# A fused decoder layer in float32: laying out the staging tiles of the up and the down projection, and ending the sums of the down weights earlier

## The chip, the cores and the metric

The kernel runs on one core of a Trainium2 chip. The metric is the device time of one execution of the whole layer in microseconds (us), lower being better. Six actors matter below: TensorE (PE, the matrix products), VectorE (DVE), ScalarE (ACT), GpSimd (POOL), SyncE (SP, which here only issues transfers), and the 16 DMA engines that carry the transfers. Each engine works through its own list of instructions in order and stands at the first one whose condition isn't met.

## The reference

One layer of a decoder for 2048 tokens of width 1024, all in float32. What the change touches is the gated MLP in the middle of it; the lines ahead of it write the `h` that it reads.

```python
h = h + jnp.concatenate([att, pool], axis=-1) @ w_out[i]      # output projection
hn = _rmsnorm(h, ln_ffn[i])
up = _causal_dwconv(hn @ w_up[i], conv_w[i], conv_b[i])       # up stage, 1024 -> 2 x 2816
gate, val = jnp.split(up, 2, axis=-1)
h = h + (jax.nn.silu(gate) * val) @ w_down[i]                 # down stage, 2816 -> 1024
g = jax.nn.sigmoid(_rmsnorm(h, ln_ple[i]) @ w_ple_gate[i])    # gate stage
h = h + g * (p[i] @ w_ple[i])
```

## The kernel before

**Products.** Every float32 operand is split into a high part (a cast on ACT, L84) and a low part (a subtraction on DVE, L85), and a product is three passes of PE: high by high, high by low, low by high (L89 to L91). Both projections of the MLP further save an eighth of the products by a scheme of seven products of half size in place of eight; its operands are sums and differences of quarters of the matrices, named `a11`, `a12`, `a22`, `s1` to `s4` on the side of the activations and `b11`, `b21`, `b22`, `t1` to `t4` on the side of the weights.

**Output projection.** It runs ahead of the up stage. Its mix tiles (`mh`, `ml`) are the moving operand of the products `o` (L89 to L91); the last group walks eight steps `k`, twelve products to a step. Its staging tiles `xc` (tag `xh1`) take the new `h` and are written out to memory.

**Up stage.** It has 44 turns of about 19 us: 2 halves of the tokens times 22 column blocks `f`. A turn makes seven products of twelve matmuls each (L1395), into the PSUM banks `ua`, `ub` and `uc`; the last of a turn is `s4`, and the product `a22` of a turn is made at the head of the next, ahead of that turn's `s2`. The program is written turn by turn, and within the `with tc.manual_schedule` block all engines execute in the order of the text. What stands in it besides the products:

- `raw_load` (L1061, L1065) fetches the weights of a turn as two raw tiles on SP's queue; the second of them lies in the tile `raw2`.
- `Refill.fetch` (L1435) loads operands that an earlier stage left in memory, into `nt` and `ninv` tiles, also on SP's queue; `Refill.take` (L1451, L1452) splits them on ACT and DVE. At the head of the stage six such loads, for `a12` and `s3`, stand right behind the raw weights of turn 1.
- Conv, Silu and the multiplication with the other half (`yv`, `uv`, `ug`, `yg`, L1661 for the multiplication) run one turn behind the products. `results` writes the quarter sums out; `x` and `x2` are its temporaries in tag `dg`. `keep` (L1478) puts most of these writes on SP, the last turn's on GpSimd.
- `down_sums` (L1518) makes, for each of 11 `q`, four sums of the down weights on GpSimd, an operation and a write each (L1530, L1531); the down stage reads them from memory. They are spread over the later turns, by slots, of which a turn has seven.
- `first_units` (L1462, L1465) prepares the first five units of the down stage inside the last turns, from tiles of the up stage's own pools.

**Down stage.** 154 units: 2 halves times 7 products times 11 `q`. A unit needs one weight tile `rw` (L1710) and one activation tile `ra` (L1712), 256 KB each, loaded on SP's queue, and the splits of both (`w` tiles, `ah`, `al`; L84, L85); then PE makes 12 products `dn`. `ahead` loads and splits up to four units beyond the present one, with four buffers of `rw` and of `ra` and seven of `ah` and `al`. The old `h` tiles are loaded by GpSimd (L1756) and the finished sums added to them on DVE (L1764). Only PE's order is that of the text here; the loop is the scheduler's otherwise.

**Where tiles lie.** A tile pool hands out memory by tags: all tiles of a tag share a fixed number of rotating buffers, and the tags of a pool lie one behind the other in the order in which they are first asked for. A pool that opens where an earlier one closed takes over its bytes, and with `reuse_waits="tile"` each new tile then waits for the last users of the very bytes that it lies on, not for the whole old pool. So the place of a tag decides what its first tiles wait for. A tile named `first`, asked for and not used, fixes the place of its tag. Three pools follow each other on the same bytes: the one of the output projection, `fb` of the up stage (with `opb`, the split operands `s3`, `a22` and `a12`, behind it from the other side) and `fd` of the down stage. In KB from their common start:

| pool | tags in order, with the first KB of each |
|---|---|
| output projection | `xh1` 0, mix tiles 20, output weights (`xw`) 52, `sq` 76, `dg` 78, end 82 |
| `fb` | `halo` 0, `yv` 0.75, `uv` 4.75, `dg` 8.75, `t4` 12.75, `raw2` 14.75, `nt` 22.75, `inv` 30.75, `t13` 34.75, `ug` 38.75, `yg` 46.75, end 54.75 |
| `opb` | `s3` 55.25, `a22` 71.25, `a12` 87.25, end 103.25 |
| `fd` | `dacc` 0, `rw` 4, `ra` 12, `ah` 20, `al` 34, `h` 48, `sq` 84, `dg` 86, `inv` 90, `nt` 92, end 96 |

Of the kernel before, what the change touches and what calls it, by code (L numbers as in the profile page):

```python
# [10 lines left out]
F32 = mybir.dt.float32  # L11
F32R = mybir.dt.float32r
# [5 lines left out]
P = 128  # L18
# [7 lines left out]
NF = FF // P  # L26
CH = 512
# [939 lines left out]
def phase_rest(tc, g, mxs, mx, last_pair, xT, pT, w_out, w_up, w_down, w_gate, w_ple, outT):  # L967
# [3 lines left out]
    with ExitStack() as ctx:  # L971
# [72 lines left out]
        NP = NF // 2  # L1044
        turns = [(half, f) for half in range(2) for q in range(NP) for f in (q, q + NP)]
        fb = None
# [323 lines left out]
        fb = fctx.enter_context(tc.tile_pool(name="c_f", bufs=1, reuse_waits="tile"))  # L1370
# [3 lines left out]
        for pool, tag, n, bufs in (  # L1374
            (fb, "yv", 1024, 1),
            (fb, "uv", 1024, 1),
            (fb, "dg", CH, 2),
            (fb, "t4", CH, 1),
            (fb, "raw2", 1024, 2),
            (fb, "nt", CH, 4),  # L1380
            (fb, "inv", CH, 2),
            (fb, "t13", 1024, 1),
            (opb, "s3", CH, 8),
            (opb, "a22", CH, 8),
            (opb, "a12", CH, 8),
        ):
            pool.tile([P, n], F32R if tag == "dg" or pool is opb else F32, tag=tag, bufs=bufs, name="first")
# [123 lines left out]
        def due_sums():  # L1511
            for e in sums[:]:
                e[0] -= 1
                if e[0] < 0:
                    sums.remove(e)
                    e[1]()

        def down_sums(q):  # L1518

            b = []  # L1520
            for r in (w_down[q * P : (q + 1) * P, :], w_down[(q + NP) * P : (q + NP + 1) * P, :]):
                for x in range(2):
                    t = fb.tile([P, CH], F32, tag="nt", bufs=4, name="nt")
                    nc.gpsimd.dma_start(t, r[:, x * CH : (x + 1) * CH])
                    b.append(t)

            def one(n):
                b11, b12, b21, b22 = b
                o, x, y = ((b11, b12, b11), (b12, b22, b12), (b22, b22, b11), (b21, b21, b22))[n]
                nc.gpsimd.tensor_tensor(o, x, y, op=ALU.subtract)  # L1530
                nc.gpsimd.dma_start(g.dd[q][("t1", "t3", "t2", "t4")[n]], o)  # L1531

            return one

        with tc.manual_schedule(engines=set(EN.values())):
# [8 lines left out]
            unit = {}  # L1544
            for i in range(len(turns) + 1):
                over = i == len(turns)
# [10 lines left out]
                def after(slot):  # L1557

                    if i == 0 and 0 < slot or i == NF - 1 and slot > 0 or i in (NF, NF + 1):
                        refill.take(2 + (i == 0 and slot == 1))  # L1560
                    if i == 3 and slot == 4:
                        prep.extend(prepare(1, fb, prep, 4))
                    if prep and (i == 3 or (i, slot) == (4, 0) or (7 * i + slot) % 3 == 0):
                        prep.pop(0)()
                    m = 7 * (i - NF - 2) + slot
                    if m >= 0 and not over:
                        q, at = divmod(m, 14) if m < 14 * (NP - 2) else (i - 2 * NF + NP, slot)
                        wide = m < 14 * (NP - 2)
                        if at == 0:
                            unit["sum"] = down_sums(q)  # L1570
                        for x in range(4):
                            if at == ((2, 5, 8, 11) if wide else (2, 3, 4, 5))[x]:
                                unit["sum"](x)
                    due_sums()

                def splits(slot):
# [12 lines left out]
                if prev:  # L1589
                    nc.scalar.copy(prev.uv[:, lo_], prev.a)  # L1590
                    prev.yv = fb.tile([P, 1024], F32, tag="yv", name="yv")
                    conv_a(prev.yv, prev.uv, NF + prev.f)
                after(0)
                keep_t(i + 1)

# [9 lines left out]
                if over:  # L1605
                    unit[3]()
                after(1)
                if last:
                    for n in range(2):
# [5 lines left out]
                if prev and not over:  # L1615
                    add(prev.ug[:, hi_], prev.c)
                splits(2)
                after(2)
                if last:
                    unit[0]()  # L1620
# [61 lines left out]
        psd = dctx.enter_context(tc.tile_pool(name="c_psd", bufs=1, space=PSUM, reuse_waits="tile"))  # L1682
        fd = dctx.enter_context(tc.tile_pool(name="c_fd", bufs=1, reuse_waits="tile"))
        aux[0] = fd

        SEQ = (
            ("a11", "b11", True, True, (0, 0)),
# [237 lines left out]
def tile_layer(ctx, tc, xT, pT, vec, w_in, pool_w, w_out, w_up, w_down, w_gate, w_ple, near_b, far_b, rcnt, outT, upto=9):  # L1925
# [44 lines left out]
    with tc.manual_schedule(engines={mybir.EngineType.PE}):  # L1970
        with tc.manual_schedule(engines={EN[e] for e in ACFG["man"]}):
            phase_project(tc, g, xT, w_in, pool_w, rcnt)
        if upto > 1:
            mxs = ExitStack()
            mx = mxs.enter_context(tc.tile_pool(name="b_mx", bufs=1, side="right", reuse_waits="tile"))
            last = phase_attention(tc, g, mx, near_b, far_b)
            if upto > 2:
                phase_rest(tc, g, mxs, mx, last, xT, pT, w_out, w_up, w_down, w_gate, w_ple, outT)
            else:
                mxs.close()  # L1980
# [71 lines left out]
```

## Time and profile before

| | us |
|---|---|
| median of 3 runs | 2386.14 |
| lowest and highest of them | 2383.86, 2395.26 |
| the profiled execution, its own time | 2386.58 |
| its span in the profile | 2384.8 |
| stages in it: up to the up stage | 0 to 848.5 |
| up stage | 848.5 to 1703 |
| down stage | 1703 to 2144 |
| gate stage and the rest | 2144 to 2384.8 |

The profile is that of one execution. Its mean granted TensorE clock is 0.988 of full speed. A row of the timeline gives start and length of an instruction, its engine, its line, what it writes and reads, and in brackets how long the engine stood idle just before it and what it waited for. In the list of waits a row gives engine and line, what ended the wait, and the sum, the count and the longest of these waits. An arrow `out<-in` names tiles as the program does; the table above says where they lie.

### The profile page before, as it was taken

The page shows a single profiled execution, that of the slowest core. Times are in us where ns is not written, and L with a number is a line of the kernel's source. Part 1 is how long each engine was busy: PE and PEld are TensorE (multiplying, and loading weights), DVE is VectorE, ACT ScalarE, POOL GpSimd, SP SyncE. Part 2 cuts the span into 40 slices and gives each one's busy share as a digit, 9 for nine tenths or more (in the row PEclk, how much of TensorE's full clock was granted, in tenths as well). Part 3 has the DMA queues.
Part 4 walks back from the last instruction along what each step waited for, and adds up shares of the span by engine and source line. Part 5 has one row for each costly group of instructions (what it writes and reads, how often), then busy time and mean ns, then how long its engine had stood idle before and what let it go on. Part 6 is the DMA issues. An engine that isn't in the chain of part 4 may idle for free.

```text
span 2384.8 us, 32817 instructions
## 1 busy us (share of the span) xinstructions
PE 2313.2 (97%) x11279; PEld 1959.1 (82%) x11279; DVE 1705.3 (72%) x2681; ACT 1127.3 (47%) x2044; POOL 564.8 (24%) x544
## 2 busy tenths in 40 slices
PE   8999999999989999999999999999799999999998
PEld 7988888888868878888887888888678888888888
DVE  6735527888963768999999989777665666655664
ACT  5423325888821344444447445444354444444332
POOL 2312221356600223343330665000100000001000
PEclk9999999999999999999999999999999999999999
DMA  8635346697575754656567777443497776754332
GB/s 261 206 119 190 150 166 243 226 258 256 152 254 191 233 197 144 209 187 209 203 204 253 268 278 252 156 147 130 152 316 231 236 247 196 236 166 149 119 102 94
DMA packets 240552, 476.01 MB, mean 200 GB/s; under 512 B 37472, under 2 KB 63904, under 8 KB 237312
## 3 DMA queue, kind: packets, MB, share of 16 engines
q1 hardware_dynamic: 205040, 394.64, 49.8%
q0 software_dynamic: 15696, 51.49, 6.1%
q10 hardware_dynamic: 19648, 27.77, 3.3%
q8 instruction: 89, 1.46, 0.3%
q14 instruction: 79, 0.65, 0.1%
HBM read 309.14 MB, written 156.79 MB: 195 GB/s over the span
## 4 chain that ended last, share of the span: by engine, by line
PE 86%; DVE 5%; DMA 4%; issue 2%; ACT 1%; POOL 0%; SPq 0%; ACTq 0%; DVEq 0%; POOLq 0%
PE ua L1395 18%; PE uc L1395 9%; PE dn L89 6%; PE dn L90 6%; PE dn L91 6%; PE ub L1395 5%; PE z L90 5%; PE z L89 5%; PE z L91 4%; PE o L91 2%; PE o L89 2%; PE o L90 2%; PE gp L89 2%; PE gp L91 2%; PE gp L90 2%
## 5 line engine op out<-in xcount | busy, mean ns | idle before, releaser
L89 PE MATMUL dn<-ah,wu 128*128 128x512 f32 x616 | 241.4, 392 | 13.2 <-ACT ah L84 13.2
L90 PE MATMUL dn<-al,wu 128*128 128x512 f32 x616 | 241.1, 391 | 1.7 <-DVE al L85 1.7
L91 PE MATMUL dn<-ah,wu 128*128 128x512 f32 x616 | 240.7, 391 | 0.0
L85 DVE TENSOR_TENSOR al<-ra,ah 128x512 fp32r<-128x512 f32 x154 | 106.0, 690 | 128.9 <-ACT ah L84 128.7
L89 PE MATMUL z<-hnh,wh 128*128 128x512 f32 (+1 forms) x480 | 168.7, 351 | 8.0 <-ACT hnh L258 6.3
L84 ACT CAST ah<-ra 128x512 fp32r<-128x512 f32 x154 | 95.2, 620 | 166.5 <-PE dn L91 144.6
L90 PE MATMUL z<-hnl,wh 128*128 128x512 f32 (+1 forms) x480 | 168.2, 350 | 0.1
L91 PE MATMUL z<-hnh,wl 128*128 128x512 f32 (+1 forms) x480 | 167.8, 350 | 0.0
L89 PEld LDWEIGHTS dn<-ah,wu 128*128 128x128 f32 x616 | 116.3, 189 | 37.7 <-ACT ah L84 13.6
L90 PEld LDWEIGHTS dn<-al,wu 128*128 128x128 f32 x616 | 116.3, 189 | 26.9 <-DVE al L85 2.6
L91 PEld LDWEIGHTS dn<-ah,wu 128*128 128x128 f32 x616 | 116.3, 189 | 24.2
L85 DVE TENSOR_TENSOR wu<-ru,wu 128x1024 fp32r<-128x1024 f32 x88 | 134.7, 1530 | 2.0 <-ACT wu L84 2.0
L1395 PE MATMUL ub<-a12h,wu 128*128 128x512 f32 x352 | 117.5, 395 | 2.4 <-ACT a12h L1451 2.4
L1395 PE MATMUL ua<-s1h,wu 128*128 128x512 f32 x352 | 115.7, 390 | 0.8 <-ACT ug L1626 0.8
L1395 PE MATMUL ua<-s2h,wu 128*128 128x512 f32 x352 | 115.7, 390 | 0.8 <-ACT ug L1600 0.7
L1395 PE MATMUL uc<-s3h,wu 128*128 128x512 f32 x352 | 115.6, 389 | 0.0
L1395 PE MATMUL uc<-a22h,wu 128*128 128x512 f32 x352 | 115.6, 389 | 0.0
L1395 PE MATMUL ua<-s4h,wu 128*128 128x512 f32 x352 | 115.5, 389 | 0.0
L1395 PE MATMUL ua<-a11h,wu 128*128 128x512 f32 x352 | 115.5, 389 | 0.0
L85 DVE TENSOR_TENSOR wu<-rw,wu 128x512 fp32r<-128x512 f32 x149 | 100.8, 686 | 15.6 <-ACT wu L84 15.6
L89 PEld LDWEIGHTS z<-hnh,wh 128*128 128x128 f32 x480 | 92.5, 193 | 20.0 <-ACT hnh L258 6.3
L89 PE MATMUL o<-mh,hwo 128*128 128x512 f32 x256 | 101.4, 396 | 5.8 <-ACT hwo L84 5.8
(337 smaller groups left out, 6621.4 us busy)
## 6 DMA issues: line engine op xcount, KB each, us to landing
ru<-in_w_up_dram SPq DMA_DIRECT2D x66, 512.0 KB, 4.0
wr<-in_w_in_dram SPq DMA_DIRECT2D x64, 256.0 KB, 5.0
rw<-in_w_down_dram SPq DMA_DIRECT2D x61, 256.0 KB, 3.9
nt<-h SPq DMA_DIRECT2D x56, 256.0 KB, 3.8
td<-t SPq DMA_DIRECT2D x22, 512.0 KB, 2.6
t<-td SPq DMA_DIRECT2D x22, 512.0 KB, 3.7
nt<-in_w_down_dram POOLq DMA_DIRECT2D x44, 256.0 KB, 5.5
ra<-oq0s SPq DMA_DIRECT2D x44, 256.0 KB, 3.2
```

What stands on the lines that cost most here:

```text
L84: nc.scalar.copy(hi, src)
L85: (low or nc.gpsimd).tensor_tensor(lo, src, fp(hi), op=ALU.subtract)
L89: nc.tensor.matmul(ps, wh, ah, start=first, stop=False, skip_group_check=again)
L90: nc.tensor.matmul(ps, wh, al, start=False, stop=False, skip_group_check=again)
L91: nc.tensor.matmul(ps, wl, ah, start=False, stop=last, skip_group_check=again)
L1395: nc.tensor.matmul(pst, x[:, ksl], y, start=first and k == 0 and n == 0, stop=k == HK - 1 and n == 2, skip_group_check=True)
```

## The change

Three edits. In `fb` the tag `yg` moves from the end to behind `uv`, so that `dg`, `t4`, `raw2`, `nt`, `inv`, `t13` and `ug` lie 8 KB further back. In `fd` all tags are given a fixed order, with `h` first. And a down weight's four sums take 12 slots instead of 14, for all 11 `q` alike, so that in the text the sums end about a turn sooner.

| pool | tags in order after the change, with the first KB of each |
|---|---|
| `fb` | `halo` 0, `yv` 0.75, `uv` 4.75, `yg` 8.75, `dg` 16.75, `t4` 20.75, `raw2` 22.75, `nt` 30.75, `inv` 38.75, `t13` 42.75, `ug` 46.75, end 54.75 |
| `fd` | `h` 0, `dacc` 36, `inv` 40, `nt` 42, `sq` 46, `dg` 48, `ah` 52, `rw` 66, `ra` 74, `al` 82, end 96 |

```diff
             (fb, "yv", 1024, 1),
             (fb, "uv", 1024, 1),
+            (fb, "yg", 1024, 2),
             (fb, "dg", CH, 2),
...
-                    m = 7 * (i - NF - 2) + slot
-                    if m >= 0 and not over:
-                        q, at = divmod(m, 14) if m < 14 * (NP - 2) else (i - 2 * NF + NP, slot)
-                        wide = m < 14 * (NP - 2)
+                    q, at = divmod(7 * (i - NF - 2) + slot, 12)
+                    if 0 <= q < NP:
                         if at == 0:
                             unit["sum"] = down_sums(q)
-                        for x in range(4):
-                            if at == ((2, 5, 8, 11) if wide else (2, 3, 4, 5))[x]:
-                                unit["sum"](x)
+                        if at in (2, 5, 8, 10):
+                            unit["sum"]((2, 5, 8, 10).index(at))
                     due_sums()
...
         aux[0] = fd
+        for tag, n, bufs in (
+            ("h", CH, 18),
+            ("dacc", CH, 2),
+            ("inv", CH, 1),
+            ("nt", CH, 2),
+            ("sq", CH, 1),
+            ("dg", CH, 2),
+            ("ah", CH, 7),
+            ("rw", CH, 4),
+            ("ra", CH, 4),
+            ("al", CH, 7),
+        ):
+            fd.tile([P, n], F32R if tag in ("ah", "al", "dg") else F32, tag=tag, bufs=bufs, name="first")
```

The sequence of instructions is the same on every engine before and after. What differs is the waits that the rows carry in brackets: the names there are counters, of an engine's work (PE, DVE, Activation) or of the transfers of a queue (DMAHW for the hardware queues, DMASW for those of GpSimd). SP's list at the start of the down stage, before; `rd` and `oq0a` are the last prepared unit's weight and the kept results:

```order
L1462 DMA rd<-in_w_down_dram 128x512 [waits DMAHW4_49,DMAHW2_49,DVE_49]
L1710 DMA rw<-in_w_down_dram 128x512 [waits DMAHW3_49,DVE_49]
L1712 DMA ra<-oq0a_210 128x512 [waits DMASW5_49,DVE_49]
L1710 DMA rw<-in_w_down_dram 128x512 [waits DMAHW5_49,DMASW2_49]
L1712 DMA ra<-oq0a_211 128x512 [waits DMAHW6_49]
```

The same place after the change, whose lines stand 11 further down here:

```order
L1463 DMA rd<-in_w_down_dram 128x512 [waits DMAHW4_49,DMAHW2_49,DVE_49]
L1721 DMA rw<-in_w_down_dram 128x512 [waits DMAHW3_49,PE_49]
L1723 DMA ra<-oq0a_210 128x512 [waits PE_49]
L1721 DMA rw<-in_w_down_dram 128x512 [waits DMAHW5_49]
L1723 DMA ra<-oq0a_211 128x512 [waits DMAHW6_49]
```

The first `rw` and the first `ra` no longer wait for DVE and GpSimd's transfers, but for PE. SP's list at the start of the up stage, before; `ru` is the second raw weight tile of turn 1 (in `raw2`), `op0a` and `op0s` hold the operands of the refill:

```order
L1065 DMA ru_9244<-in_w_up_dram 128x1024 [waits DMAHW3_49,DMAHW4_49,DMAHW2_49,Activation_49]
L1435 DMA nt<-op0a_131 128x512 [waits DMAHW5_49,PE_49]
L1435 DMA nt<-op0a_132 128x512 [waits DMAHW6_49,PE_49]
L1435 DMA nt<-op0a_133 128x512 [waits DMAHW7_49]
```

And after:

```order
L1065 DMA ru_9245<-in_w_up_dram 128x1024 [waits DMAHW4_49,PE_49]
L1436 DMA nt<-op0a_131 128x512 [waits DMAHW5_49,PE_49]
L1436 DMA nt<-op0a_132 128x512 [waits DMAHW6_49]
L1436 DMA nt<-op0a_133 128x512 [waits DMAHW7_49]
```

Here too the raw tile's waits for several queues and ACT have become one queue's and PE's.

## The prediction

> **What bounds the kernel now.** I read the page first: TensorE is busy for all but 72 us of the span.
>
> ```profile
> PE 2313.2 (97%) x11279; PEld 1959.1 (82%) x11279; DVE 1705.3 (72%) x2681; ACT 1127.3 (47%) x2044; POOL 564.8 (24%) x544
> ```
>
> So a change that leaves the products alone can only win back gaps of PE, or time in which PE runs below full clock. The second view is the table by stretches (columns: length, busy time and count of PE, PEld, DVE, ACT and POOL, granted clock, DMA share, GB/s), cut where the up stage begins (848.5), where the down stage begins (1703) and where both have settled.
>
> ```profile
> 848.50:881.00 32.50, 28.37 (x110) 20.86 (x109) 22.95 (x26) 18.00 (x28) 12.81 (x8) 0.89 0.75 262
> 881.00:1703.00 822.00, 818.11 (x3604) 675.69 (x3603) 730.47 (x798) 410.63 (x506) 254.71 (x209) 1.00 0.59 198
> 1703.00:1760.00 57.00, 42.09 (x171) 33.64 (x170) 33.68 (x51) 22.05 (x36) 13.91 (x26) 0.85 0.78 281
> 1760.00:2144.00 384.00, 384.00 (x1707) 318.22 (x1706) 234.86 (x371) 180.84 (x314) 12.39 (x20) 1.00 0.69 222
> ```
>
> The two starts are the two places in these stages where both PE time and clock are missing; behind each start PE is full at clock 1.00, so what a start wins is not given back there. The list of waits names what PE stood on, and the list of SyncE's queue (SPq) what held the loads behind that.
>
> ```profile
> PE dn L89 <- ACT ah L84: 13.2, 1, 13.2
> PE ub L1395 <- ACT a12h L1451: 2.4, 1, 2.4
> PE dn L90 <- DVE al L85: 1.7, 1, 1.7
> ```
>
> ```profile
> SPq L1710 <- DVE yg L1661: 12.6, 1, 12.6
> SPq L1712 <- DMA oq1s<-x: 10.9, 1, 10.9
> ...
> SPq L1065 <- DMA h<-xc: 12.2, 1, 12.2
> ```
>
> None of the three SP waits is for data. In-order SP holds the first `rw` (L1710) until DVE has done the last `yg` product (L1661), because `rw` lies on the bytes of `yv` and `uv`; the first `ra` (L1712) until the sum `x2` has been written out, because it lies on `dg` and `t4`; and at the up stage's start the second raw weight tile (L1065) until the last `x` tiles of the output projection have been written out. All six operand loads stand behind that one in the queue.
>
> **The down stage's start.** The timeline (start, length, engine, line, instruction; idle time before it in brackets):
>
> ```profile
> 1684.08 2.72 PE uc L1395 x12
> ```
>
> ```profile
> 1715.97 0.50 PE L90 MATMUL dn<-al,wu 128*128 128x512 f32 x1 [1.75 <-DVE al L85]
> ...
> 1718.37 0.39 PE L91 MATMUL dn<-ah,wu 128*128 128x512 f32 x1
> 1731.93 0.79 PE L89 MATMUL dn<-ah,wu 128*128 128x512 f32 x1 [13.16 <-ACT ah L84]
> ...
> 1738.56 0.40 PE L89 MATMUL dn<-ah,wu 128*128 128x512 f32 x1
> ```
>
> Twelve products take 2.72 us, 0.2267 each; that is one unit (one `rw`, one `ra`). Units 0 to 4 come from the up stage's own tiles and end at 1718.37 + 0.23 = 1718.60. Unit 5 begins at 1731.93: 13.33 us lost. From there to 1738.56 stand 15 products in 6.63 us instead of 3.40: 3.23 us lost to the clock. Together 16.56.
>
> Why unit 5 is late, from SP's timeline, the chain and ACT's timeline:
>
> ```profile
> 1700.24 0.33 SPq L1462 DMA_DIRECT2D rd<-in_w_down_dram  x1
> 1713.29 0.33 SPq L1710 DMA_DIRECT2D rw<-in_w_down_dram  x1
> 1724.57 0.33 SPq L1712 DMA_DIRECT2D ra<-oq0a  x1
> ```
>
> ```profile
> 1724.57 6.66 DMA ra<-oq0a
> ```
>
> ```profile
> 1731.26 0.62 ACT L84 CAST ah<-ra 128x512 fp32r<-128x512 f32 x1 [14.27 <-DMA ra<-oq0a]
> ...
> 1734.27 0.62 ACT L84 CAST ah<-ra 128x512 fp32r<-128x512 f32 x1 [1.11 <-DMA ra<-oq0a]
> ...
> 1737.84 0.62 ACT L84 CAST ah<-ra 128x512 fp32r<-128x512 f32 x1 [1.23 <-DMA ra<-oq0a]
> ...
> 1741.45 0.62 ACT L84 CAST ah<-ra 128x512 fp32r<-128x512 f32 x1 [1.16 <-DMA ra<-oq0a]
> ```
>
> With the new layout `rw` lies over `s3`, whose first tiles PE last reads in the product that ends before `s4`, and `ra` over `a22`, last read by the up stage's last product, which ends where the stage does, about 1703. SP's order is unchanged, so the first `rw` goes right behind the `rd` at 1700.24, near 1700.6, and the first `ra` near 1703.2; the other six loads of the first four units have no wait of their own and follow about 0.4 us apart, to 1706. Even with the 6.66 us of this row they land by 1713. What is late next is DVE, whose order is also unchanged:
>
> ```profile
> 1717.76 0.68 DVE L85 TENSOR_TENSOR wu<-rw,wu 128x512 fp32r<-128x512 f32 x1
> ```
>
> The split of unit 5's weight ends at 1718.45 and that of its activation, 0.6 later, at 1719.05; PE's second product of unit 5 wants it at 1718.83. That is a new wait of about 0.25 us. The wait of 1.75 for unit 4 stays, since it hangs on the last turn's conv and Silu on DVE and ACT, which do not move. The clock loss goes with the long gap. Gain here 16.56 - 0.25 = 16.3 us.
>
> A cost comes from the reads of `h`. They now lie over `halo` to `nt`, are issued by GpSimd behind the last results as before, and meet the loads of units 9 and up.
>
> ```profile
> 1720.05 2.13 POOL L1756 DMA_DIRECT2D h<-h  x4 [1.38 <-DMA oq1s<-yg]
> ...
> 1735.84 0.54 POOL L1756 DMA_DIRECT2D h<-h  x1 [0.43 <-DMA h<-h]
> ```
>
> While these ran, the four casts above came 3.0, 3.6 and 3.6 us apart, 3.4 on average, against the 2.72 that PE needs. After the change unit 9's loads go out at about 1718.5, when unit 5's splits free their buffers, and land by 1725.2; with two splits (0.6 and 0.7) it is ready at 1726.5. PE wants it at 1718.85 + 4 x 2.72 = 1729.7: a lead of 3.2 us, used up at 0.7 a unit after five units, about when the burst ends. I put the cost at 0 to 2 us and take 1, since the lead and the burst end nearly together. [...]
>
> **The up stage's start.**
>
> ```profile
> 848.63 0.39 PE L91 MATMUL o<-mh,lwo 128*128 128x512 f32 x1
> ```
>
> ```profile
> 855.03 0.39 PE L1395 MATMUL ua<-s2h,wu 128*128 128x512 f32 x1
> 857.84 0.80 PE L1395 MATMUL ub<-a12h,wu 128*128 128x512 f32 x1 [2.42 <-ACT a12h L1451]
> ...
> 864.58 0.40 PE L1395 MATMUL ua<-s1l,wu 128*128 128x512 f32 x1
> ```
>
> ```profile
> 852.75 0.33 SPq L1065 DMA_DIRECT2D ru<-in_w_up_dram  x1
> 853.17 1.81 SPq L1435 DMA_DIRECT2D nt<-op0a  x4
> ```
>
> ```profile
> 857.17 0.62 ACT L1451 CAST a12h<-nt 128x512 fp32r<-128x512 f32 x1 [4.81 <-DMA nt<-op0a]
> ```
>
> PE could go on at 855.03 + 0.23 = 855.26 and goes on at 857.84: 2.58 us. Then 13 products take 6.74 us instead of 2.95: 3.79 more. Together 6.37. In the new layout `raw2` lies over mix tiles that PE last reads seventh of eight in the output projection's last group, free one step of 12 products before the end, at 848.86 - 2.72 = 846.1, and `nt` over tiles read up to the last of those products, 848.9. So the `nt` loads go out at about 849.0 instead of 853.17. With the 4.0 us that the first took before (853.17 to 857.17) it lands at 853.0; cast and split end near 854.4, before 855.26. It may be 0.9 us later before PE waits. The writes of the last `x` tiles share that time, so the bounds of this gain are 0 and 6.37, and I take 6.4. Behind it the chain that runs from PE's `st` products over ACT to DVE keeps its distance from PE.
>
> ```profile
> 858.00:860.00 2.00, 2.00 (x4) 0.95 (x4) 1.70 (x2) 1.87 (x4) 1.92 (x2) 0.50 1.03 319
> ...
> 1714.00:1716.00 2.00, 0.25 (x3) 0.03 (x1) 1.97 (x4) 0.00 (x0) 1.98 (x5) 1.00 0.78 244
> ```
>
> These two stretches price short gaps: the one of 2.58 us was followed by clock 0.50, the one of 1.75 was not. [...]
>
> **The sums of the down weights** move in the text of the program only. On each of the five engines the instructions stand in the same sequence as before, because GpSimd already runs its sums as fast as buffers allow:
>
> ```profile
> 1480.28 0.56 POOL L1531 DMA_DIRECT2D dd10t<-nt  x1 [0.30 <-POOL nt L1530]
> ```
>
> ```profile
> 1758.99 0.33 SPq L1710 DMA_DIRECT2D rw<-dd0t  x1
> ```
>
> The last sum leaves at 1480 and the first is read at 1759. I cost this edit at nothing; 278 us of cover would have to go first. The gate stage's tiles now lie over `h` instead of `rw` and `ah`, and wait for the last writes of the down stage:
>
> ```profile
> 2145.38 0.33 ACTq L1767 DMA_DIRECT2D h<-h  x1
> ```
>
> The gate's products need the sums in these same tiles for their norm anyway, so I put down nothing for that wait.
>
> **The sum.** 16.3 - 1.0 + 6.4 = 21.7 us. The profiled execution took 2386.58 us (its span and 1.78 around it), 0.44 above the median of 2386.14. 2386.58 - 21.7 = 2364.9, and against the median 2364.5.
>
> **Rivals.**
> A, as above: 2364.5, chance 0.58.
> B, only the down start comes: the operand loads at 849 queue behind the `x` writes, PE still waits over 2 us for `a12` and loses its clock. For it: the DMA share in that stretch is 0.75 already. Against it: 0.9 us of room. 2364.5 + 6.4 = 2371, chance 0.15.
> C, PE catches up with the transfers: during the `h` burst a gap opens that is long enough for the clock. Priced like the gap seen, 2.6 + 3.8 = 6.4 less the 1.0 already counted: 2370, chance 0.10.
> D, the clock falls at what is left: the 1.75 us for unit 4 and the 0.25 behind it come 3 us apart. It costs 3.2 to 3.8: 2368, chance 0.08. [...]
> Two of B, C and D together: 2375 to 2378, chance 0.05.
> E, the bytes are free earlier but something else in front of the loads holds SP, and nothing changes: 2386, chance 0.02. The `rd` at 1700.24 speaks against it: SP is free then.
> F, slower: DVE adds the first `h` tiles in front of unit 16's splits.
>
> ```profile
> 1753.48 2.47 DVE L1764 TENSOR_TENSOR h<-h,dn 128x512 f32<-128x512 f32 x4
> ```
>
> If an `h` load now waits for results that leave late, DVE stands there, unit 16 is not split and PE runs dry. PE wants unit 16 at 1718.85 + 11 x 2.72 = 1748.8. The loads were issued from 1720 on; each us later than about 1747 costs one, and only from 1747 + 21.7, near 1769, would the kernel be slower, over 0.5% from 1781, where it would stand at 2398. Nothing that they wait for is that late: chance 0.02.
>
> **How the numbers follow.** Half a per cent, 12 us, is about what a measurement of this kernel can tell from no change: 2374.2 divides faster from the same. A, B, C and D lie below it, 0.91; the pairs and E within, 0.07; F above, 0.02. The range runs from 2361 (no burst cost, 2363.5, and the spread of the runs) to 2372 (B, with a little more of the burst).
>
> **What would show it.** Right: PE's 13.2 us wait for `ah` gone and 1731.93 moved to about 1719; the first `ra` issued within 1 us of the up stage's last product; clock 1.00 through both starts; first `a12` cast before 854. Wrong in part: PE waits between units 9 and 15, or half clock behind the unit 4 wait. Wrong altogether: the first `rw` and `ra` still more than 10 us behind the last up product.

## The result and the profile after

Seven runs of the changed kernel have a median of 2372.49 us (2367.64 to 2377.56), seven of the kernel before 2386.24 (2383.86 to 2395.26). The ratio of their means is 0.9932, with a 95% interval of 0.9913 to 0.9951: 16 us faster, 12 to 21 by the interval; the two medians are 13.75 us apart. The forecast was 21.7 us, and the median lies half a us above the upper end of the forecast's range, 2372. The profiled execution has a span of 2372.3 us against 2384.8.

The table by stretches of the changed kernel, with the same cuts and columns as before:

```profile
848.50:881.00 32.50, 28.38 (x111) 21.59 (x110) 25.03 (x27) 17.50 (x28) 13.00 (x8) 0.89 0.81 271
1703.00:1760.00 57.00, 54.79 (x237) 43.97 (x236) 37.53 (x57) 26.39 (x43) 13.93 (x26) 1.00 0.89 317
```

The second row is the forecast come true: the down stage's start went from 171 products at clock 0.85 to 237 at 1.00. The first row is the forecast gone wrong: the up stage's start has the same PE time and the same clock, 0.89, as before. What PE waits for at the down stage's start, from its timeline:

```profile
1717.76 0.50 PE L90 MATMUL dn<-al,wu 128*128 128x512 f32 x1 [1.75 <-DVE al L85]
1740.32 0.50 PE L90 MATMUL dn<-al,wu 128*128 128x512 f32 x1 [0.22 <-DVE al L85]
1743.78 0.50 PE L90 MATMUL dn<-al,wu 128*128 128x512 f32 x1 [0.23 <-DVE al L85]
```

The 13.2 us for `ah` are gone, the 1.75 for unit 4 has stayed, and two short waits are new. SP's timeline shows the loads:

```profile
1702.02 0.33 SPq L1463 DMA_DIRECT2D rd<-in_w_down_dram  x1
1702.45 0.41 SPq L1721 DMA_DIRECT2D rw<-in_w_down_dram  x1
1704.94 0.33 SPq L1723 DMA_DIRECT2D ra<-oq0a  x1
```

This execution stood 1.8 us later than that of before when it got here; less that, they are the forecast's 1700.2, 1700.6 and 1703.2. The up stage's start, from PE's timeline:

```profile
858.45 0.50 PE L1396 MATMUL ub<-a12l,wu 128*128 128x512 f32 x1 [0.40 <-DVE a12l L1453]
867.47 0.49 PE L1396 MATMUL uc<-s3h,wu 128*128 128x512 f32 x1 [1.18 <-ACT s3h L1452]
868.19 0.50 PE L1396 MATMUL uc<-s3l,wu 128*128 128x512 f32 x1 [0.23 <-DVE s3l L1453]
869.08 0.50 PE L1396 MATMUL uc<-s3h,wu 128*128 128x512 f32 x1 [0.16 <-ACT s3h L1452]
870.53 0.80 PE L1396 MATMUL uc<-s3l,wu 128*128 128x512 f32 x1 [0.94 <-DVE s3l L1453]
```

The 2.42 us wait for `a12` has become 0.40, but nine us later PE waits four times for `s3`. What the last two `s3` tiles stood behind, from SP's and ACT's timelines:

```profile
850.90 2.30 SPq L1436 DMA_DIRECT2D nt<-op0a  x4
854.83 2.16 SPq L1436 DMA_DIRECT2D ninv<-op0s  x2
858.31 0.33 SPq L1065 DMA_DIRECT2D ru<-in_w_up_dram  x1
858.74 0.38 SPq L1096 DMA_DIRECT2D td<-t  x1
859.22 0.38 SPq L1097 DMA_DIRECT2D td<-ru  x1
859.68 2.20 SPq L1436 DMA_DIRECT2D nt<-op0s  x2
```

```profile
866.79 0.62 ACT L1452 CAST s3h<-nt 128x512 fp32r<-128x512 f32 x1 [6.12 <-DMA nt<-op0s]
```

Their loads leave at 859.68, behind turn 2's raw tile and two writes of turn 1's sums (`td`), and the first is there at 866.8. The same load and the same cast before:

```profile
860.09 1.57 SPq L1435 DMA_DIRECT2D nt<-op0s  x2
```

```profile
865.43 0.62 ACT L1451 CAST s3h<-nt 128x512 fp32r<-128x512 f32 x1 [3.59 <-DMA nt<-op0s]
```

Counted from the end of the output projection's last product (848.85 before, 850.71 here), the load leaves 9.0 us behind it instead of 11.2, but takes 7.1 us instead of 5.3. So the tile is there only 0.5 us sooner, while PE, free of its wait for `a12`, comes for it some 5 us sooner.

To see where time comes and goes, the same product is looked up in two traces and its start in the one subtracted from its start in the other. The change of this distance over a stretch is what the stretch won (minus) or lost, free of what earlier stages did in that execution (the distance at 848.7 alone ran from -1.2 to 3.0 us). Times heading the columns are those of before; us against before:

| run | 848.7 to 863.5, `a12` | 863.5 to 881, `s3` to `a22` | 1718.4 to 1745, units 5 on | 1745 to 1760, reads of `h` |
|---|---|---|---|---|
| changed kernel | -4.6 | +4.3 | -16.6 | +1.6 |
| changed kernel, again | -4.7 | +2.9 | -16.6 | +2.3 |
| up_only | -4.7 | +4.0 | -1.9 | 0.0 |
| down_only | 0.0 | +0.6 | -8.8 | 0.0 |
| sums_only | 0.0 | 0.0 | -1.0 | 0.0 |
| pad | -0.6 | -0.5 | -16.6 | +2.0 |
| deep | -4.5 | +1.8 | -16.6 | +1.9 |
| td_late | -4.5 | -0.5 | -16.6 | +3.0 |
| h_sp | -4.6 | +1.4 | -16.6 | 0.0 |
| td_h | -4.6 | -0.5 | -16.6 | 0.0 |
| best1 | -4.6 | -0.5 | -16.6 | 0.0 |
| raw_behind | -5.4 | +6.3 | -16.6 | +1.7 |
| fill | -0.6 | -0.5 | -0.9 | 0.0 |

The first row in words: 16.6 won at the down stage, 1.6 given back to the reads of `h`, and at the up stage 4.6 won and 4.3 lost again. How far one trace can be off by chance is seen where the up stage is that of before: down_only is 0.6 above it there, pad 1.1 below.

### The profile page after: what moved, and what is told of

Same layout as the page of the kernel before. It is cut to its first block, busy times and chain, and to the rows that moved or that the text cites. A ratio compares the mean times of both kernels' runs of the same rounds, so it can differ in the third digit from the quotient of the medians.

```text
span 2372.3 us, 32820 instructions
## 1 busy us (share of the span) xinstructions
PE 2312.0 (97%) x11279; PEld 1957.9 (83%) x11279; DVE 1701.3 (72%) x2681; ACT 1124.9 (47%) x2044; POOL 566.0 (24%) x544
## 4 chain that ended last, share of the span: by engine, by line
PE 85%; DVE 5%; DMA 5%; issue 2%; ACT 1%; POOL 0%; ACTq 0%; SPq 0%; DVEq 0%; POOLq 0%
PE ua L1396 19%; PE uc L1396 9%; PE dn L89 5%; PE dn L90 5%; PE dn L91 5%; PE z L89 5%; PE z L90 5%; PE ub L1396 5%; PE z L91 5%; PE o L91 2%; PE o L89 2%; PE o L90 2%; PE gp L89 2%; PE gp L91 2%; PE gp L90 2%
## 5 line engine op out<-in xcount | busy, mean ns | idle before, releaser
L155 DVE TENSOR_TENSOR acc<-acc,sq 128x512 f32<-128x512 f32 (+1 forms) x118 | 79.1, 671 | 41.8 <-ACT sq L154 30.7
```

Source lines behind the costliest of these rows:

```text
L155: nc.vector.tensor_tensor(acc[:, :n], acc[:, :n], sq[:, :n], op=ALU.add)
```

## The experiments

Each is timed against the kernel before; unless said otherwise the edit stands on the changed kernel.

**The parts alone.** The first puts only the list of the down stage's tags into the kernel before, the second only the `yg` line, the third only the new slots of the sums.

```diff
+        for tag, n, bufs in (
+            ("h", CH, 18),
...
+            fd.tile([P, n], F32R if tag in ("ah", "al", "dg") else F32, tag=tag, bufs=bufs, name="first")
```

> The kernel before with the fixed order of the down stage's tiles alone. Theory (the down stage's start is the whole gain): the wait of 13.2 us and the half clock behind it go, two short waits come back during the reads of h, and the time is 15 us below before, near 2371. Rival (the parts need each other, since the up stage's shift also moves what the down tiles lie on): less than 10 us.

Measured: 2379.32 us, ratio 0.9971 (0.9960 to 0.9981), 7 us and not 15. The list of waits and ACT's timeline:

```profile
PE dn L89 <- ACT ah L84: 4.9, 1, 4.9
```

```profile
1725.26 0.62 ACT L84 CAST ah<-ra 128x512 fp32r<-128x512 f32 x1 [9.40 <-DMA oq1s<-yg]
```

The loads leave as early as in the full change (the first `ra` at 1705.45), and the weight is cast at 1715. But the activation's cast into `ah` waits 9.4 us for a write out of `yg`: in the new order `ah` lies from 52 KB on, and in the old layout of the up stage `yg` ends at 54.75. So the rival was right, and the `yg` line, which the prediction had filed under the up stage, is needed here.

```diff
             (fb, "uv", 1024, 1),
+            (fb, "yg", 1024, 2),
```

> The kernel before with yg moved forward in the up stage's pool alone. Theory (the earlier a12 only moves the wait to the last two s3 tiles, which come no earlier): within 2 us of before; PE reaches s3 about 4.5 us earlier and has lost it all by the end of turn 0. Rival (the clock loss at s3 was a chance of one execution): 4 to 6 us faster than before, no half clock behind s3.

Measured: 2385.97 us, ratio 1.0001 (0.9993 to 1.0010). As the theory said, the wait moved from `a12` to `s3`:

```profile
PE uc L1396 <- ACT s3h L1452: 2.4, 2, 2.3
...
PE ub L1396 <- DVE a12l L1453: 0.4, 1, 0.4
```

```diff
+                    q, at = divmod(7 * (i - NF - 2) + slot, 12)
+                    if 0 <= q < NP:
...
```

> The kernel before with the 12-slot schedule of the down weights' sums alone. Theory (same sequence on every engine): same as before within 2 us. Rival (GpSimd's earlier sums take VectorE's time or the transfers'): 2 us or more away from before, and a shift that grows over the turns between 1280 and 1480 us.

Measured: 2387.22 us, ratio 1.0004 (0.9994 to 1.0014): nothing. This execution did lose 2.0 us to before between 1276 and 1491, where the sums run, as the rival had it. But over the same stretch the nine traces with the new slots lost 0.1 to 3.1 us to the trace of before, and the four others with the old slots between -0.1 and 3.1. So these losses come with either schedule, and the times show none of it; a difference under a us between the schedules is not excluded.

**Is it `ah` over `yg`?** The run with the down list alone, with two tiles of 2 KB that nobody uses ahead of `ah`:

```diff
+            ("pad", CH, 2),
             ("ah", CH, 7),
```

> The run with the down stage's order alone, plus 4 KB left empty ahead of ah, so that ah lies behind yg's old place; the up stage's layout is that of before. Theory (with the down order alone, ScalarE's cast into ah waits for the writes out of yg, on whose bytes it lies, and that is all that the yg line brings): the 4.9 us wait for ah and its half clock go too, 15 us below before, near 2371. Rival (the yg line helps the down stage in another way, by the turns before it): it stays at 2378 to 2380.

Measured: 2372.4 us, ratio 0.9941 (0.9928 to 0.9953). PE's list of waits in the down stage:

```profile
PE dn L90 <- DVE al L85: 2.2, 3, 1.7
PE dn L89 <- ACT ah L84: 0.2, 1, 0.2
```

4 KB of empty space do all at the down stage that the `yg` line does: -16.6 us again. All of the change's gain is at the down stage, and it hangs on where three tags lie.

**Why `s3` comes late.** First the last two `s3` tiles were loaded ahead of need, into a tile of `ug` that turn 0 leaves free:

```diff
...
+            t = fb.tile([P, 1024], F32, tag="ug", bufs=2, name="ug")
+            refill.more = [t[:, lo_], t[:, hi_]]
+            refill.fetch()
+            refill.fetch()
             sums_t(1)
```

> The changed kernel with the third and fourth s3 tile loaded ahead, right behind the first six operand tiles, into the half of ug that turn 0 doesn't use. Theory (PE loses at s3 what it won at a12, because these two loads stand behind the a12 splits and the writes of td in SP's queue): their casts come before 862 instead of 866.8, the four waits at s3 (2.5 us) and the half clock behind them go, 4.7 us less than the changed kernel, near 2368. Rival (the 16 DMA engines are full there, so that a load issued earlier only delays another): a12 lands later instead, PE waits there over 2 us, and nothing is gained.

Measured: 2372.29 us, ratio 0.9944 (0.9932 to 0.9956), no less than the changed kernel. The casts came at 862.8 and 866.1, the waits at `s3` went down to one, but the next operand took over, and the clock fell again: the product `s4` needs a copy on ACT (`uv`), which stands behind the cast of an `a22` tile that landed at 868.7. PE's timeline and the table by stretches:

```profile
868.12 0.50 PE L1396 MATMUL uc<-s3l,wu 128*128 128x512 f32 x1 [0.71 <-DVE s3l L1460]
869.84 0.50 PE L1396 MATMUL ua<-s4h,wu 128*128 128x512 f32 x1 [0.99 <-ACT uv L1656]
```

```profile
870.80:874.20 3.40, 3.40 (x10) 2.62 (x9) 3.40 (x3) 2.96 (x5) 2.12 (x2) 0.50 0.73 269
```

The theory was half right: 2.5 of the 4.3 us are won in this one trace, too little to be timed. Then the queue itself: the writes of turn 1's sums go behind all operand loads of turn 0.

```diff
-                keep_t(i + 1)
+                if i != 0:
+                    keep_t(i + 1)
...
                 after(3)
+                if i == 0:
+                    keep_t(1)
+                    keep_t4(1)
```

> The changed kernel with the three writes of turn 1's sums (td) moved behind the operand loads in SP's queue. Theory (the third and fourth s3 tile come late because they stand behind these writes in the queue and share the engines with their 768 KB): their casts come 1.5 to 3 us sooner than 866.8, and turn 0 ends 1.5 to 4 us earlier against the changed kernel. Rival (they are late because their buffers come free only with the a12 splits): casts within 1 us of 866.8, nothing gained.

Measured: 2369.0 us, ratio 0.9923 (0.9908 to 0.9938). This execution stood 3.0 us earlier than the changed kernel's at 848.7. SP's and PE's timelines:

```profile
855.56 0.92 SPq L1436 DMA_DIRECT2D nt<-op0s  x2
...
859.14 0.54 SPq L1096 DMA_DIRECT2D td<-t  x1
```

```profile
865.03 0.49 PE L1396 MATMUL uc<-s3l,wu 128*128 128x512 f32 x1 [0.72 <-DVE s3l L1453]
```

The casts of the two tiles come at 861.0 and 863.0 instead of 866.8 and 868.4; with the 3.0 taken off, 2.8 and 2.4 us sooner. Of the 2.8, 1.1 is the earlier start of the load and 1.7 its shorter way, 5.4 us instead of 7.1. PE has one short wait at `s3`, no half clock, and of the 4.6 us won at `a12` nothing is lost: -5.0 over the whole start. Buffers were not what held these loads; their place behind the `td` writes was, in SP's queue and among the transfers under way.

**Why `a12` was split later than forecast.** The first `a12` tile was split by 858.4, 7.7 us behind the end of the last product of the output projection (850.7 in this execution), and not 5.5. DVE's timeline of the changed kernel, and of a run in which turn 1's raw weights are loaded behind the six operand tiles, so that GpSimd's sums of them start later:

```diff
-            raw_load(1)
             refill = Refill(0, ("a12", "s3", "a22"), 6)
             for _ in range(6):
                 refill.fetch()
+            raw_load(1)
```

> The changed kernel with turn 1's raw weights loaded behind the six operand tiles instead of ahead of them. Theory (VectorE's additions into acc take 1.5 to 1.6 us instead of 0.7 because GpSimd's sums of the raw weights, which now start 4.7 us earlier, run beside them, and that holds the a12 splits): the additions are back at 0.7, the first a12 split starts 5 us behind the last o product instead of 6.8, and the s3 tiles come earlier by as much. Rival (the additions are slow because transfers fill the memory there): they stay at 1.5.

```profile
852.12 5.68 DVE L155 TENSOR_TENSOR acc<-acc,sq 128x512 f32<-128x512 f32 x4
```

```profile
850.95 3.07 DVE L155 TENSOR_TENSOR acc<-acc,sq 128x512 f32<-128x512 f32 x4
854.39 0.69 DVE L1453 TENSOR_TENSOR a12l<-nt,a12h 128x512 fp32r<-128x512 f32 x1 [0.36 <-ACT a12h L1452]
```

Four additions take 5.68 us beside GpSimd's sums and 3.07 without: three of them last 1.5 to 1.6 us, and 0.69 alone. Each of the three ends 0.55 us behind the end of one of GpSimd's sums (853.07, 854.74 and 856.45). The split then ends at 855.08, 5.5 us behind the last product (849.55 here), which is the forecast's number. The theory holds, as far as the times go: 1.5 to 1.6 us beside GpSimd's sums, 0.69 alone. By what means a sum on GpSimd holds up an addition on DVE was not shown. As a change it does not pay: 2375.8 us, ratio 0.9941 (0.9923 to 0.9959). The third `s3` tile was cast 3.1 us sooner, measured from the last product, but the next wait grew, for a copy on ACT that stands behind the cast of a late `a22` tile:

```profile
871.20 0.79 PE L1396 MATMUL ua<-s4h,wu 128*128 128x512 f32 x1 [3.02 <-ACT uv L1645]
```

**What half clock costs.** Into the kernel before, ten products that nobody reads were put into the 2.6 us for which PE waits for `a12`. If it is this gap that brings the clock down, the clock now stays up; if it is the full transfers, half clock comes as before. I looked for a time 0 to 4 us below that of before.

```diff
                     cur.b = bank("ub")
+                    if i == 0:
+                        for _ in range(10):
+                            nc.tensor.matmul(cur.b, W[0, "b21"][0][:, :P], A["s2"][0][0], start=True, stop=True, skip_group_check=True)
```

> The kernel before with ten extra products of PE put into the wait of 2.58 us for a12 in turn 0; their sums are overwritten by the real product, so the output is unchanged. [...]

Measured: 2385.26 us, ratio 0.9996 (0.9986 to 1.0006). The stretch and PE's timeline:

```profile
855.00:865.00 10.00, 8.12 (x33) 5.55 (x32) 5.69 (x6) 4.20 (x7) 4.66 (x3) 1.00 1.01 359
```

```profile
858.25 0.50 PE L1395 MATMUL ub<-a12l,wu 128*128 128x512 f32 x1 [0.23 <-DVE a12l L1452]
859.94 0.50 PE L1395 MATMUL ub<-a12l,wu 128*128 128x512 f32 x1 [0.73 <-DVE a12l L1452]
861.63 0.50 PE L1395 MATMUL ub<-a12l,wu 128*128 128x512 f32 x1 [0.73 <-DVE a12l L1452]
```

The clock stays at 1.00, against 0.66 in the same stretch before, while the transfers are as full as before (DMA share 1.01 in this stretch in both), so the gap is what brings it down. But of the 3.79 us that the prediction had booked as lost to the clock only 1.1 are won: at full clock PE waits for each `a12` tile in turn. I had expected PE to reach `s3` 3.8 us sooner, and that failed.

**The reads of `h`.** SP issues them between the units' loads, one behind a pair, instead of GpSimd all at once:

```diff
-            if x in (0, 2, 3, 6) and q in (2, 4, 6, 8):
-                j = (q - 2) // 2
+            if x in (0, 2, 3, 6) and q in (6, 7, 8, 9):
+                j = q - 6
...
-                nc.gpsimd.dma_start(ht, g.h1[4 * col + j][:, c * CH : (c + 1) * CH])
+                nc.sync.dma_start(ht, g.h1[4 * col + j][:, c * CH : (c + 1) * CH])
```

> The changed kernel with the reads of h issued by SP between the loads of the units, each behind one unit's pair, instead of by GpSimd in one burst. Theory (the burst takes the transfers from the units 9 to 16): the two waits near 1740 and the 1.4 us behind them go, and nothing else moves; 1 to 2 us less than the changed kernel. Rival (transfers are as full either way): the same 1.4 us is lost, or more where SP stands for an h buffer.

Measured: 2369.4 us, ratio 0.9925 (0.9912 to 0.9939). ACT's casts of the units' activations, in the changed kernel and then in this run:

```profile
1731.25 0.62 ACT L84 CAST ah<-ra 128x512 fp32r<-128x512 f32 x1 [1.03 <-DMA ra<-oq0a]
...
1734.77 0.62 ACT L84 CAST ah<-ra 128x512 fp32r<-128x512 f32 x1 [1.06 <-DMA ra<-oq0a]
...
1738.92 0.62 ACT L84 CAST ah<-ra 128x512 fp32r<-128x512 f32 x1 [1.65 <-DMA ra<-oq0a]
```

```profile
1730.61 0.62 ACT L84 CAST ah<-ra 128x512 fp32r<-128x512 f32 x1
...
1732.68 0.62 ACT L84 CAST ah<-ra 128x512 fp32r<-128x512 f32 x1
...
1734.59 0.62 ACT L84 CAST ah<-ra 128x512 fp32r<-128x512 f32 x1
```

Units come 3.5 and 4.2 us apart during GpSimd's burst and 2.0 without it; PE needs 2.72. The edit also spreads the reads: GpSimd had issued 18 of them by 1736.5, SP issues four by 1728.3 and the next at 1756.9. So the run shows that the burst is the cause, and not whether the issuing engine matters. The two short waits and the 1.6 us behind them are gone in all three runs with this edit.

**Both repairs.** `td` behind the operands and `h` by SP, with the `s3` tiles loaded further ahead (best1) and without (td_h), and the changed kernel once more.

> The changed kernel with the s3 tiles loaded ahead, the td writes behind the operand loads, and h read by SP. Theory: the waits at s3 and s4 of turn 0 go with the half clock behind them, and so does the loss during the reads of h: 5 to 6 us less than the changed kernel, near 2367. Rival (the next operand, a22, or ScalarE's order holds PE and drops the clock again): 1 to 3 us less, near 2370.

> The changed kernel with the td writes of turn 0 behind the operand loads and h read by SP, without the deeper prefetch. Theory (the first repairs the up stage's start, 5 us, the second the 1.5 us of the reads of h, and loading s3 further ahead adds nothing): within 1.5 us of the run with all three, near 2367, 5 to 6.5 us less than the changed kernel beside it. Rival (the two repairs take transfers from each other or from later turns): less than 3 us.

> The changed kernel once more, beside the others on the same chip, as the base of their comparison: 2370 to 2374. [...]

Measured: best1 2367.42 us, ratio 0.9915 (0.9901 to 0.9928); td_h 2367.63, ratio 0.9913 (0.9900 to 0.9926); beside td_h on the same chip the changed kernel again 2372.34, ratio 0.9931 (0.9918 to 0.9944). Five runs of td_h lie between 2365.63 and 2370.87, five of the changed kernel between 2369.70 and 2374.29. So td_h is 4.7 us faster than the changed kernel by the medians, though the ranges touch, and clearly faster than the kernel before; loading `s3` further ahead adds nothing to it that these runs could tell. The three profiles with the up stage's code of the changed kernel (its first, this second and h_sp's) show two, one and no stretch of 3.41 us at half clock at `s3`.

## Why the prediction was right and wrong

**Right: the down stage's start.** The 16.56 us booked there came as 16.6 in every trace that has both layouts. The 0.25 us set against it for a wait behind unit 4 did not come. But the step that told why was incomplete: it followed `rw` and `ra` over the bytes that they now lie on and forgot `ah`. With `yg` in its old place half of the gain is missing; the prediction gave that line to the up stage only.

**Right in kind: the reads of `h`.** Booked at 1.0 us, between 0 and 2, they cost 1.6 to 3.0 in six executions (over 2 in two of them), through short waits at full clock. Rival C, a gap long enough for the clock, did not occur.

**Wrong: the up stage's start.** The step that failed is the last of its working: behind `a12` it followed only the chain from PE's `st` products over ACT to DVE, said that this keeps its distance from PE, and booked the whole 6.4 us; the loads of `s3` it put at nothing without a reason. The loads of `nt` did go out with the end of the last product, and PE won 4.6 us at `a12`. But the loads of the next operand kept their place behind the `td` writes and landed at most 1.1 us sooner, and PE lost 4.3, 4.0, 2.9 and 1.4 us again in four executions of the same code there. Nor did the chain named keep its distance: ACT's first step of it (`ms`) started 3.5 us behind the first `st` product instead of 1.0, since it stands in ACT's list behind the cast of a late `s3` tile. So what came was near the number of rival B, 2371, which had a chance of 0.15, by another mechanism: B had `a12` itself late. A smaller miss is the split that ended 7.7 us behind the last product and not 5.5, through GpSimd's sums, which start as early as the raw tile lands.

**Wrong: the price of half clock.** 2.58 us of waiting plus 3.79 of slow products were added up as if both were to be had. The run with the filled gap shows 1.1 of the 3.79: half clock hides the wait for the tiles that follow. The same sum was right at the down stage, where the new layout brings the units behind the first forward as well.

**Right: the sums of the down weights, and no slower case.** Rivals D and F did not occur: behind unit 4's wait of 1.75 us the clock stayed at 1.00 in all nine traces with the new start. For D there may have been luck in it: at `s3` half clock came behind 3.41 us in which PE was idle for 1.66, and near 1295, in six of fourteen traces, behind a single pause of 1.9 us (both by the last section).

With the terms as measured the changed kernel comes to 16.6 - 1.6 + 0.3 = 15.3 us by its own trace, inside the interval of 12 to 21; the forecast of 21.7 is just outside it, and 6.1 of the 6.4 us between the two sums are the up stage's.

## What to carry to other kernels

When a wait at a stage's start is taken away, follow the queue that feeds it on to the second and third operand: what those stand behind has not moved. When a tile is moved, look at what every tag of the new pool lies over, also those that an engine writes, not only those that transfers fill. And before a stretch of slow clock is booked as gain, ask whether its operands were there.

## What the runs showed of the hardware

The clock came down behind shorter waits than the 2.58 us that the prediction had priced: none of the four at `s3` is longer than 1.18. The table by stretches of the changed kernel, cut where the clock changes:

```profile
866.27:869.68 3.41, 1.75 (x5) 0.67 (x4) 2.24 (x3) 2.89 (x6) 1.35 (x1) 1.00 0.82 300
869.68:876.50 6.82, 5.97 (x14) 4.73 (x15) 6.82 (x8) 4.32 (x7) 4.11 (x3) 0.50 0.55 187
```

In the 3.41 us ahead of the fall PE is busy for 1.75 and idle for 1.66; half clock then lasts 6.82, and in the run with the deeper prefetch 3.40. PE's timeline of the run with `h` read by SP has nearly the same four waits at `s3`, and no fall:

```profile
866.50 0.49 PE L1396 MATMUL uc<-s3h,wu 128*128 128x512 f32 x1 [0.63 <-ACT s3h L1452]
867.23 0.50 PE L1396 MATMUL uc<-s3l,wu 128*128 128x512 f32 x1 [0.23 <-DVE s3l L1453]
868.12 0.49 PE L1396 MATMUL uc<-s3h,wu 128*128 128x512 f32 x1 [0.16 <-ACT s3h L1452]
869.57 0.50 PE L1396 MATMUL uc<-s3l,wu 128*128 128x512 f32 x1 [0.95 <-DVE s3l L1453]
```

Here 1.97 us of waiting are spread over 3.7 us, there 2.51 over 4.2.

Another place shows that the length of the wait alone does not decide. In one turn near 1295 all fourteen traces have a single pause of 1.9 us at `s4`. In six of them half clock follows; in the other eight the clock stays at 1.00. The changed kernel has one execution of each kind. PE's timeline and the table by stretches of its first:

```profile
1297.88 0.50 PE L1396 MATMUL ua<-s4l,wu 128*128 128x512 f32 x1 [1.94 <-DVE s4l L1453]
```

```profile
1296.33:1299.74 3.41, 1.86 (x8) 1.55 (x9) 3.41 (x6) 3.34 (x5) 0.00 (x0) 1.00 0.47 111
1299.74:1303.15 3.41, 3.41 (x17) 2.80 (x16) 3.41 (x5) 2.28 (x4) 0.00 (x0) 1.00 0.82 309
```

And of its second:

```profile
1293.48 0.50 PE L1396 MATMUL ua<-s4l,wu 128*128 128x512 f32 x1 [1.91 <-DVE s4l L1453]
```

```profile
1291.22:1294.63 3.41, 1.50 (x7) 0.96 (x6) 3.41 (x7) 2.91 (x4) 0.00 (x0) 1.00 0.40 129
1294.63:1298.04 3.41, 3.41 (x10) 2.62 (x9) 3.41 (x6) 1.03 (x3) 0.00 (x0) 0.50 0.77 292
```

The pause of 1.94 us was followed by clock 1.00 and the one of 1.91 by 0.50; what decides between the two was not shown. At `s3` the executions differ too: with two, one and no stretch at half clock the changed kernel's code lost 4.3, 2.9 and 1.4 us there, though the waits differ a little too. Near 1295 the fall cost next to nothing: between 1276 and 1319 both executions of the changed kernel lost 0.1 us to before, because at half clock the waits that follow at full clock (0.1 and 0.9 us) did not occur.
